# Tile-by-tile memory hand-over, early activation loads and a ScalarE permutation in a two-layer hybrid encoder

## The chip, the cores and the metric

The kernel runs on 1 core of one Trainium2 chip. The metric is the device time of one execution in microseconds (us). Traces come from the hardware profiler of that core. TensorE's clock has two granted levels, 2.4 GHz (1.00 in the tables) and 1.2 GHz.

## What is computed

Sixteen learned meta tokens are put ahead of 512 tokens, 528 in all, of width 2048, float32. Two layers follow, each with an RMSNorm in front and a residual add behind, and a last RMSNorm. Cut to what matters:

```
def even_layer(h, ...):
    proj = rmsnorm(h) @ w_in                     # 2048 x 12352
    z_a, xs, Bm, Cm, dt_f, dt_b, z_b, glu_v, glu_g = split_cols(proj)
    y_a = ssd_mixer(...)                         # conv 5, two-way chunked scan, gate z_a, norm
    y_b = conformer_conv(glu_v, glu_g) * silu(z_b)   # conv 31, LayerNorm
    return h + concat(y_a, y_b) @ w_out          # 4096 x 2048

def odd_layer(h, ...):
    q, k, v, z = split(rmsnorm(h) @ w_in)        # 2048 x 8192
    o = neighbourhood_attention(q, k, v, rpb)    # 8 rows x 64 columns, window 16 columns
    return h + (o * silu(z)) @ w_out             # 2048 x 2048
```

The attention layer keeps its tokens with the column of the grid first and the row second, so the first layer's result is permuted once, from (row, column) to (column, row).

## The kernel before, in words

Activations lie with the channels on the 128 partitions, 16 tiles of 128 x 528 per layer. Every product is computed to float32 accuracy by three matmuls: weights and activations are split into a rounded high part and a rest (`wh`, `wl`; `rh`, `rl`), and high x high, low x high and high x low are accumulated. `fetch` (line 214) splits a weight half-panel of 128 x 1024, ScalarE for `wh` (line 221), DVE for `wl` (line 224); weights are loaded by SP (line 145) into three buffers `raw`, and three split halves are kept ahead. `split` (line 277) makes `rh` on ScalarE and `rl` on DVE; the results live in a ring of 16 tiles each, so a new stage's tile k takes the place of the old stage's tile k.

The program is a row of stages:

- an input stage with the SSD heads (to about 1060 us), then the gate stage of lines 613 to 662: 16 panels of `z_b`, whose loop runs beside the LayerNorm of `ln` (line 623). Its tiles lie in the pools `zbp` (14 tiles), `big` (16) and `rp`; each product `xc` is stored to `yb_d`.
- three calls of `phase` (line 808): the output projection of `y_a` (from `yz_d`), that of `y_b` (from `yb_d`, with `done_b` at line 862, which adds the residual, permutes the tokens and stores to `h1_d`), and the q, k, v projection (from `h1_d`). A phase fills the ring by `fill` (line 696), does four panels by `proj`, and the rest two panels at a time as 7 half-size products instead of 8 by `sproj` (line 232), for which `combos` (line 713) makes sums of activation halves, `ta` and `tb`; these sums need the same 16 tiles a second time. `fourth` (line 735) replaces one half of the ring from `t4_d`.
- The phases' pools are opened at lines 684 to 688: `sr` with 8 tiles, through which every streamed activation, residual and fourth block passes (`stream`, line 690), `tr` for `ta` and `tb`, `wx` for weight sums `wy` and `wb`, and `ev` for results `cx`, `cy`. The first `fill` issues on SP, later streams on POOL.
- the attention stage (lines 917 to 1189), pools `ak` and `ap`: 16 head pairs, with the panels of the gate `z` interleaved in chunks (`chunks`, `filler`), and, in the last two pairs, with `reload` (line 1087) of the first twelve gated outputs from `o_d` and `refill` (line 1099), which splits them into the ring.
- the output stage (from line 1182), pools `op`, `fp` and `wf`: the last projection with its own `combos` (line 1192), whose inputs `srf` share seven buffers `rr` with the residuals, then the last norm and the store.

A pool of a later stage takes the memory of an earlier one. Before the change every instruction that first uses a pool waits until the pools whose memory it takes are done with all their tiles. Across most of the program the order on each engine is planned by the framework from a simulated time line, and instructions move far from where they are written; in the attention stage the order on TensorE, DVE, ScalarE and POOL is the written one (`manual_schedule`), while SP's DMA issues are still planned. Each engine's queue runs in order.

Of the kernel before, what the change touches and what calls it, by code (L numbers as in the profile page):

```python
# [12 lines left out]
F32 = mybir.dt.float32  # L13
# [4 lines left out]
P = 128  # L18
# [42 lines left out]
SRB = 8  # L61
# [17 lines left out]
def hybrid_encoder(ctx: ExitStack, tc: tile.TileContext, hT, win, wdt, wout, oin, oout, par, con,  # L79
# [15 lines left out]
    nc.scalar.dma_start(cst[:, CON["one"][0]:], con[:, CON["one"][0]:])  # L95

# [515 lines left out]

    with ExitStack() as c1:
        psb = c1.enter_context(tc.tile_pool(name="psc", bufs=1, space=bass.MemoryType.PSUM))
        zb = c1.enter_context(tc.tile_pool(name="zbp", bufs=14))
        big = c1.enter_context(tc.tile_pool(name="big", bufs=16))
        rp = c1.enter_context(tc.tile_pool(name="rp", bufs=1))
# [32 lines left out]
        for m in range(KT):  # L650
# [5 lines left out]
            if bgc:  # L656
                pump(bgc, 7000)
                if not bgc:
                    bgs.append(ln())
            else:  # L660
                pump(bgs, 7000)
        pump(bgs, 1e9)
# [20 lines left out]
    with ExitStack() as c1:  # L683
        sr = c1.enter_context(tc.tile_pool(name="sr", bufs=SRB))
        wx[1] = c1.enter_context(tc.tile_pool(name="pse", bufs=4, space=bass.MemoryType.PSUM))
        tr = c1.enter_context(tc.tile_pool(name="tr", bufs=KH))
        wx[0] = c1.enter_context(tc.tile_pool(name="wx", bufs=1))
        ev = c1.enter_context(tc.tile_pool(name="ev", bufs=1))

        def stream(src, q=nc.gpsimd):  # L690
            t = sr.tile([P, L], F32, name="srt", tag="srt")
            if src is not None:
                q.dma_start(t, src)
            return t

        def fill(src, g, q=nc.gpsimd):
            hs, ls = [], []
            for k in range(KT):
                t = src(k) if k in near else stream(src(k), q)
# [35 lines left out]
        def fourth(hs, ls):  # L735
            ts = deque()
            for k in range(0, KH + 4, 2):
                now = [ts.popleft() for _ in range(2 if k >= 4 else 0)]
                for kk in range(k, min(k + 2, KH)):
                    t = sr.tile([P, L], F32, name="sr4", tag="srt")  # L740
# [121 lines left out]
        def done_b(m, t, ps):  # L862
# [5 lines left out]
            if t is None:  # L868
                t = ev.tile([P, L], F32, name="cx", tag="xy", bufs=3)
                nc.scalar.activation(h2(t), ps, AF.Copy)  # L870
            nc.vector.tensor_tensor(r1[:, :NM], t[:, :NM], r0[:, :NM], op=ALU.add)
            nc.vector.tensor_tensor(r1[:, NM:].rearrange("p (c r) -> p r c", r=GR), t[:, NM:].rearrange("p (r c) -> p r c", r=GR),
                                    r0[:, NM:].rearrange("p (r c) -> p r c", r=GR), op=ALU.add)
# [43 lines left out]
    wx[0] = None  # L917
    pstack.close()
    psp[0] = pstack.enter_context(tc.tile_pool(name="pz", bufs=2, space=bass.MemoryType.PSUM))

    with ExitStack() as c2:
# [184 lines left out]
        with tc.manual_schedule(engines={eng.PE, eng.DVE, eng.Activation, eng.Pool}):  # L1106
# [15 lines left out]
            for p in range(KT):  # L1122
# [47 lines left out]
                if p == KT - 2:  # L1170
                    refill(0, 4)
# [234 lines left out]
```

## Time and profile before

| | us |
|---|---|
| three runs | 2688.16, 2694.21, 2695.9 (median 2694.21) |
| the profiled execution | 2690.2 |
| its span, first to last instruction | 2688.4 |
| TensorE busy | 2620.0 (97%) |
| DVE busy | 2056.2 (76%) |
| ScalarE busy | 1399.4 (52%) |
| POOL busy | 395.4 (15%) |

Times in the rows count from the start of the span. PE is TensorE's matmuls, PEld its weight loads, ACT ScalarE, SP the queue of SyncE, which only issues DMAs. Matmuls are pipelined, so the busy time of one overlaps the next: a gap between two starts says more than a sum of durations. What ended an idle time is inferred from semaphores.

### The profile page before, as it was taken

The page shows a single profiled execution, that of the slowest core. Times are in us where ns is not written, and L with a number is a line of the kernel's source. Part 1 is how long each engine was busy: PE and PEld are TensorE (multiplying, and loading weights), DVE is VectorE, ACT ScalarE, POOL GpSimd, SP SyncE. Part 2 cuts the span into 40 slices and gives each one's busy share as a digit, 9 for nine tenths or more (in the row PEclk, how much of TensorE's full clock was granted, in tenths as well). Part 3 has the DMA queues.
Part 4 walks back from the last instruction along what each step waited for, and adds up shares of the span by engine and source line. Part 5 has one row for each costly group of instructions (what it writes and reads, how often), then busy time and mean ns, then how long its engine had stood idle before and what let it go on. Part 6 is the DMA issues. An engine that isn't in the chain of part 4 may idle for free.

```text
span 2688.4 us, 52587 instructions
## 1 busy us (share of the span) xinstructions
PE 2620.0 (97%) x21228; PEld 2499.3 (93%) x21228; DVE 2056.2 (76%) x3019; ACT 1399.4 (52%) x2601; POOL 395.4 (15%) x608
## 2 busy tenths in 40 slices
PE   8999999999999999999899999999999999999997
PEld 7999999999999999999899989999999987777797
DVE  7775967888587969987588888877777766666776
ACT  5355585655658655225454445633333455566443
POOL 2000000000000001101121212200000042442432
PEclk9999999999999999999999999999999999999998
DMA  4222222232222223434776767755555453543764
GB/s 162 96 75 92 84 78 95 79 99 74 89 87 73 90 89 100 156 103 143 249 215 194 250 186 244 239 159 157 158 149 155 143 152 119 142 124 108 244 185 151
DMA packets 145156, 375.50 MB, mean 140 GB/s; under 512 B 32512, under 2 KB 45472, under 8 KB 144912
## 3 DMA queue, kind: packets, MB, share of 16 engines
q1 hardware_dynamic: 121296, 292.68, 33.8%
q0 software_dynamic: 23328, 79.38, 11.0%
q8 instruction: 167, 2.74, 0.4%
q14 instruction: 77, 0.63, 0.1%
q10 hardware_dynamic: 288, 0.07, 0.0%
HBM read 321.64 MB, written 50.43 MB: 138 GB/s over the span
## 4 chain that ended last, share of the span: by engine, by line
PE 79%; DMA 6%; DVE 6%; ACT 5%; issue 3%; POOL 1%; SPq 0%; DVEq 0%; POOLq 0%; ACTq 0%
PE ps L266 40%; PE pb L245 25%; PE ps L1059 6%; PE py L537 2%; DVE wl L224 1%; PE po L1045 1%; ACT wh L221 1%; DMA srt<-yz_d 1%; PE st L477 1%; DVE a L560 1%; PE pq L996 1%; DMA t_d<-srt 1%; DMA srt<-yb_d 1%; ACT T L505 1%; ACT L507 1%
## 5 line engine op out<-in xcount | busy, mean ns | idle before, releaser
L266 PE MATMUL ps<-rh,wh 128*128 128x264 f32 (+1 forms) x3520 | 732.2, 287 | 21.3 <-ACT rh L283 17.4
L266 PE MATMUL ps<-rh,wl 128*128 128x264 f32 (+1 forms) x3520 | 732.3, 287 | 0.4 <-DVE wl L224 0.4
L266 PE MATMUL ps<-rl,wh 128*128 128x264 f32 (+1 forms) x3520 | 727.6, 287 | 1.9 <-DVE rl L284 1.3
L221 ACT ACTIVATE wh<-raw 128x1024 fp32r<-128x1024 f32 (+1 forms) x341 | 360.4, 1057 | 530.7 <-PE ps L266 278.8
L266 PEld LDWEIGHTS ps<-rh,wh 128*128 128x128 f32 (+1 forms) x3520 | 550.5, 189 | 28.6 <-ACT rh L283 18.4
L224 DVE TENSOR_TENSOR wl<-raw,wh 128x1024 fp32r<-128x1024 f32 (+1 forms) x341 | 432.4, 1268 | 165.6 <-ACT wh L221 160.3
L266 PEld LDWEIGHTS ps<-rl,wh 128*128 128x128 f32 (+1 forms) x3520 | 547.4, 188 | 6.6 <-DVE rl L284 2.9
L266 PEld LDWEIGHTS ps<-rh,wl 128*128 128x128 f32 (+1 forms) x3520 | 550.4, 188 | 3.0 <-DVE wl L224 0.9
L245 PE MATMUL pb<-rh,wh 128*128 128x264 f32 (+1 forms) x1280 | 364.1, 285 | 1.3 <-DVE fo L1290 1.3
L245 PE MATMUL pb<-rl,wh 128*128 128x264 f32 (+1 forms) x1280 | 363.7, 284 | 0.0
L245 PE MATMUL pb<-rh,wl 128*128 128x264 f32 (+1 forms) x1280 | 363.0, 284 | 0.4 <-DVE wl L224 0.4
L560 DVE SCALAR_TENSOR_TENSOR a<-up,prm,a 128x528 f32<-128x528 f32 x464 | 343.9, 771 | 2.4 <-ACT a L555 1.0
L245 PE MATMUL pb<-ta,wh 128*128 128x264 f32 (+1 forms) x1280 | 241.4, 286 | 9.2 <-ACT wh L221 3.9
L245 PEld LDWEIGHTS pb<-rh,wh 128*128 128x128 f32 x1280 | 241.0, 188 | 2.4 <-DVE fo L1290 2.4
L245 PEld LDWEIGHTS pb<-rh,wl 128*128 128x128 f32 x1280 | 240.7, 188 | 0.8 <-DVE wl L224 0.8
L245 PEld LDWEIGHTS pb<-rl,wh 128*128 128x128 f32 x1280 | 240.9, 188 | 0.0
L245 PEld LDWEIGHTS pb<-ta,wh 128*128 128x128 f32 x1280 | 200.9, 190 | 11.3 <-ACT wh L221 4.9
L221 ACT ACTIVATE wh<-wy 128x1024 fp32r<-128x1024 f32 x117 | 123.9, 1059 | 147.9 <-PE pb L245 97.3
L224 DVE TENSOR_TENSOR wl<-wy,wh 128x1024 fp32r<-128x1024 f32 x117 | 146.0, 1248 | 61.1 <-ACT wh L221 61.0
L245 PE MATMUL pb<-ta,wl 128*128 128x264 f32 (+1 forms) x640 | 183.7, 287 | 5.3 <-DVE wl L224 5.3
L221 ACT ACTIVATE wh<-wb 128x1024 fp32r<-128x1024 f32 x80 | 84.7, 1059 | 99.5 <-PE pb L245 50.0
L245 PEld LDWEIGHTS pb<-ta,wl 128*128 128x128 f32 x640 | 121.5, 190 | 7.3 <-DVE wl L224 7.3
(328 smaller groups left out, 4149.6 us busy)
## 6 DMA issues: line engine op xcount, KB each, us to landing
raw<-win SPq DMA_DIRECT2D x192, 512.0 KB, 3.6
raw<-oin SPq DMA_DIRECT2D x84, 512.0 KB, 4.5
raw<-wout SPq DMA_DIRECT2D x40, 512.0 KB, 5.5
wb<-oin SPq DMA_DIRECT2D x22, 512.0 KB, 4.0
wy<-oin SPq DMA_DIRECT2D x22, 512.0 KB, 3.4
wy<-oin POOLq DMA_DIRECT2D x22, 512.0 KB, 7.6
raw<-oout SPq DMA_DIRECT2D x20, 512.0 KB, 4.9
srt<-h_d POOLq DMA_DIRECT2D x38, 264.0 KB, 4.9
```

The lines of the kernel that those rows point to most:

```text
L221: nc.scalar.activation(wh, raw, AF.Copy)
L224: nc.vector.tensor_tensor(wl, raw, wh.bitcast(F32), op=ALU.subtract)
L245: nc.tensor.matmul(o, w[:, k, :], u[:, lo:lo + n], start=(new and k == 0 and j == 0), stop=(k == KH - 1 and j == 2), skip_group_check=not new)
L266: nc.tensor.matmul(ps[:M, n, :N], w[:, k, :], u[:, lo + n * N:lo + (n + 1) * N], start=(kk == 0 and j == 0), stop=(kk == KT - 1 and j == 2))
L477: nc.tensor.matmul(st[:, :nd * 256], xb[:, c, 256:], xd[:, d0:d1].rearrange("p r x -> p (r x)"), start=True, stop=True)
L505: nc.scalar.activation(T[:, d, c * CH:(c + 1) * CH], pf[:CH, c // 3, (c % 3) * CH:(c % 3 + 1) * CH], AF.Relu, bias=fcol[:, c, d, hd:hd + 1 ...
L507: nc.scalar.activation(h2(cq[:, d]), pf[:, :, :HL], AF.Exp)
L537: nc.tensor.matmul(py[j * HD:(j + 1) * HD, c // 3, (c % 3) * CH:(c % 3 + 1) * CH], a, b, start=(q == 0), stop=(q == nt - 1))
L560: nc.vector.scalar_tensor_tensor(a, u[:, j:j + L], wv(j), a, op0=ALU.mult, op1=ALU.add)
L996: nc.tensor.matmul(pqs[a, w][:, :n], x[hs, w * P:(w + 1) * P], y[hs, st:st + n], start=(j == 0), stop=(j == 2))
L1045: nc.tensor.matmul(self.po[hs, w * P:(w + 1) * P], lt, rt, start=(q == 0), stop=(q == nq - 1))
L1059: nc.tensor.matmul(ps, w[:, k, :], u[:, lo:lo + S], start=(kk == 0 and j == 0), stop=(kk == KT - 1 and j == 2))
```

## The change

- All pools from the gate stage on are opened with waits tile by tile: a new tile waits only for what lay under it.
- The stream pool is divided: `sr` with 5 tiles is opened ahead of the gate stage at the other end of the memory, and `sr2` with 3 at the old place; `slot` takes the eight in turn. `sr` is closed after the three phases.
- At panel 13 of 16 of the gate stage, the first five `yz_d` tiles are loaded into `sr`, on SP; `fill` finds them in `ready`.
- `done_b` adds on DVE without a permutation, in place, and ScalarE makes the two copies that permute.
- In the last pair but one, `refill(0, 4)` is divided in two and moved ahead, behind the second weight split and behind the second half of the scores.

```
-SRB = 8
+SRB, SRC = 5, 3
...
+    def pool(**kw):
+        return tc.tile_pool(reuse_waits="tile", **kw)
...
+    sstack = ctx.enter_context(ExitStack())
+    sr = [sstack.enter_context(pool(name="sr", bufs=SRB, side="right"))]
+    srn = [0]
+
+    def slot(name="srt"):
+        i = srn[0] % (SRB + SRC) if len(sr) > 1 else 0
+        srn[0] += 1
+        return sr[i >= SRB].tile([P, L], F32, name=name, tag="srt")
+
+    def stream(src, q=nc.gpsimd):
+        t = slot()
+        if src is not None:
+            q.dma_start(t, src)
+        return t
+
+    ready = {}
...
-        zb = c1.enter_context(tc.tile_pool(name="zbp", bufs=14))
-        big = c1.enter_context(tc.tile_pool(name="big", bufs=16))
+        zb = c1.enter_context(pool(name="zbp", bufs=14))
+        big = c1.enter_context(pool(name="big", bufs=16))
...
+            if m == KT - 3:
+                for k in range(SRB):
+                    ready[k] = stream(yz_d[k], nc.sync)
...
-        sr = c1.enter_context(tc.tile_pool(name="sr", bufs=SRB))
-        wx[1] = c1.enter_context(tc.tile_pool(name="pse", bufs=4, space=bass.MemoryType.PSUM))
-        tr = c1.enter_context(tc.tile_pool(name="tr", bufs=KH))
+        sr.append(c1.enter_context(pool(name="sr2", bufs=SRC)))
+        wx[1] = c1.enter_context(pool(name="pse", bufs=4, space=bass.MemoryType.PSUM))
+        tr = c1.enter_context(pool(name="tr", bufs=KH))
...
-                t = src(k) if k in near else stream(src(k), q)
+                t = src(k) if k in near else ready.pop(k) if k in ready else stream(src(k), q)
...
-                    t = sr.tile([P, L], F32, name="sr4", tag="srt")
+                    t = slot("sr4")
...
-            nc.vector.tensor_tensor(r1[:, :NM], t[:, :NM], r0[:, :NM], op=ALU.add)
-            nc.vector.tensor_tensor(r1[:, NM:].rearrange("p (c r) -> p r c", r=GR), t[:, NM:].rearrange("p (r c) -> p r c", r=GR),
-                                    r0[:, NM:].rearrange("p (r c) -> p r c", r=GR), op=ALU.add)
+            nc.vector.tensor_tensor(r0, r0, t, op=ALU.add)
+            nc.scalar.activation(r1[:, :NM], r0[:, :NM], AF.Copy)
+            nc.scalar.activation(r1[:, NM:].rearrange("p (c r) -> p r c", r=GR), r0[:, NM:].rearrange("p (r c) -> p r c", r=GR), AF.Copy)
...
+    sstack.close()
...
                 low()
+                if p == KT - 2:
+                    refill(0, 2)
                 if nxt:
                     nxt.scores((1, 2))
+                    if p == KT - 2:
+                        refill(2, 4)
                     cur.mix(o)
...
-                if p == KT - 2:
-                    refill(0, 4)
```

The remaining lines of the diff give the same `pool(...)` to `psc`, `rp`, `wx`, `ev`, `pz`, `psd`, `ak`, `ap`, `pr`, `op`, `fp`, `psf` and `wf`.

## Rows read from the trace of the kernel before

**Rows 1.** The page's parts 1 and 4: TensorE's busy time, share of the span and instructions, and the shares by engine of the chain of work that ended last.

```profile
PE 2620.0 (97%) x21228; PEld 2499.3 (93%) x21228; DVE 2056.2 (76%) x3019; ACT 1399.4 (52%) x2601; POOL 395.4 (15%) x608
...
PE 79%; DMA 6%; DVE 6%; ACT 5%; issue 3%; POOL 1%; SPq 0%; DVEq 0%; POOLq 0%; ACTq 0%
```

**Rows 2.** Busy time by stretch. The columns are the stretch in us from the span's start, its length, the busy time (and instructions) of PE, PEld, DVE, ACT and POOL, the share of TensorE's full clock that was granted, the mean busy share of the DMA engines and what they moved in GB/s.

```profile
1290.00:1299.00 9.00, 7.34 (x62) 7.18 (x60) 4.16 (x6) 2.65 (x3) 0.00 (x0) 1.00 0.21 62
...
1297.00:1372.00 75.00, 65.03 (x509) 63.73 (x508) 56.79 (x97) 46.89 (x76) 20.10 (x36) 0.95 0.87 282
...
1309.00:1340.00 31.00, 29.14 (x233) 28.41 (x233) 22.28 (x39) 21.60 (x33) 8.33 (x14) 1.00 1.00 328
...
1370.00:1460.00 90.00, 90.00 (x740) 90.00 (x739) 73.08 (x87) 34.54 (x38) 7.96 (x12) 1.00 0.62 181
...
1490.00:1536.00 46.00, 43.73 (x352) 43.06 (x353) 36.71 (x63) 20.42 (x32) 11.24 (x21) 1.00 0.77 254
...
1496.00:1680.00 184.00, 176.59 (x1408) 174.70 (x1408) 154.08 (x222) 86.96 (x123) 37.19 (x65) 0.98 0.70 219
...
1536.00:1580.00 44.00, 36.96 (x266) 35.29 (x265) 35.29 (x55) 18.85 (x30) 9.88 (x17) 0.92 0.63 198
...
2535.00:2565.00 30.00, 24.14 (x169) 22.72 (x168) 24.86 (x35) 13.81 (x23) 18.38 (x21) 0.89 0.73 226
```

**Rows 3.** Timeline around the end of the gate stage and the start of the first output projection, one row each of DVE, SP's DMA queue, ScalarE, TensorE and ScalarE again. The columns are start and duration in us, engine, line, operation, out<-in, shapes and count; in brackets the idle time before it and what ended it. Rows with a count merge several instructions.

```profile
1298.53 0.70 DVE L646 TENSOR_TENSOR xc<-xc,zb 128x528 f32<-128x528 f32 x1
...
1299.30 4.46 SPq L693 DMA_DIRECT2D srt<-yz_d  x8
...
1303.73 0.73 ACT L283 ACTIVATE rh<-srt,prm 128x528 fp32r<-128x528 f32 x1 [6.26 <-DMA srt<-yz_d]
...
1304.52 1.25 PE L266 MATMUL ps<-rh,wh 128*128 128x264 f32 x4 [7.18 <-ACT rh L283]
...
1325.96 0.74 ACT L283 ACTIVATE rh<-srt,prm 128x528 fp32r<-128x528 f32 x1 [0.38 <-DMA srt<-yz_d]
```

**Rows 4.** The second output projection: the instructions of lines 871, 872, 851 and 846 (durations are minimum/median/maximum in ns, then the first and last start in us); one row of the waits from 1536 to 1580 us (us in total, times, longest); and the row of TensorE's timeline with its longest wait there.

```profile
L871 DVE TENSOR_TENSOR srt<-cx,srt x10: 167/169/175, 1500.0 to 1670.1; 128x16 f32<-128x16 f32 x10
...
L872 DVE TENSOR_TENSOR srt<-cx,srt x10: 1144/1196/1209, 1500.0 to 1670.2; 128x512 f32<-128x512 f32 x10
...
L851 DVE TENSOR_TENSOR srt<-srt,cx x6: 701/702/703, 1378.3 to 1492.3; 128x528 f32<-128x528 f32 x6
...
L846 ACT ACTIVATE cx<-ps x4: 587/592/593, 1330.3 to 1356.8; 128x528 f32<-128x528 f32 x4
...
ACT sq L881 <- DVE srt L872: 5.6, 2, 2.8
...
1549.92 0.51 PE L245 MATMUL pb<-ta,wh 128*128 128x264 f32 x2 [2.45 <-ACT wh L221]
```

**Rows 5.** Around the change to the attention stage: timeline rows of TensorE, POOL, DVE, TensorE and DVE, and between them the stretch from 2172 to 2179 us with the columns of rows 2.

```profile
2165.54 0.28 PE L245 MATMUL pb<-ta,wl 128*128 128x264 f32 x1
...
2168.82 0.80 POOL L930 MEMSET bm<- 128x16 f32 x16 [48.05 <-PE pb L245]
...
2172.00:2179.00 7.00, 4.67 (x22) 3.57 (x21) 4.02 (x12) 2.65 (x6) 6.27 (x9) 0.76 0.99 255
...
2173.94 0.81 DVE L958 TENSOR_TENSOR ql<-tq,qh 128x512 fp32r<-128x512 f32 x1
...
2174.81 0.36 PE L996 MATMUL pq<-kh,ql 64*128 64x208 f32 x2 [2.33 <-DVE ql L958]
...
2177.28 0.38 DVE L1001 CUSTOM_DVE_ANT_0 sb<-pq,bm 128x208 f32<-128x208 f32 x1 [2.53 <-DMA vqk_d<-cy]
```

**Rows 6.** Around the last refills: the first DMA issue of line 1096 (durations in ns, first and last start in us), the stretch from 2470 to 2490 us, DVE's weight split in the timeline, two rows of the chain of work in order of time (start and duration in us, what, count), TensorE's timeline row after it, and, for comparison, a TensorE row at the start of the second output projection.

```profile
L1096 SPq DMA_DIRECT2D accl<-o_d x1: 319/319/319, 2248.2 to 2248.2; - x1
...
2470.00:2490.00 20.00, 15.05 (x103) 11.78 (x100) 14.44 (x33) 12.31 (x27) 2.95 (x2) 0.83 0.19 67
...
2469.89 1.23 DVE L224 TENSOR_TENSOR wl<-raw,wh 128x1024 fp32r<-128x1024 f32 x1 [2.07 <-ACT wh L221]
...
2473.13 0.50 ACT sb L1002 x2
...
2477.28 3.71 DVE rl L281 x4
...
2481.49 1.17 PE L1020 MATMUL pa<-cst,sb 128*128 128x128 f32 x4 [4.95 <-DVE sb L1009]
...
1495.96 0.51 PE L266 MATMUL ps<-rh,wh 128*128 128x264 f32 x2 [1.40 <-ACT rh L280]
```

**Rows 7.** Around the output stage: timeline rows of DVE, POOL, DVE and twice TensorE, and a row of the chain of work in a later stretch without a break.

```profile
2490.25 2.48 DVE L281 TENSOR_TENSOR rl<-ord,rh 128x512 fp32r<-128x512 f32 x4
...
2502.41 1.14 POOL L1237 DMA_DIRECT2D rr<-h_d  x2 [23.18 <-DMA o_d<-o]
...
2506.23 0.43 DVE L1198 TENSOR_TENSOR srf<-srf 128x256 f32<-128x256 f32 x1 [6.89 <-DMA srf<-o_d]
...
2537.65 0.39 PE L245 MATMUL pb<-ta,wh 128*128 128x256 f32 x1 [2.01 <-ACT ta L1209]
...
2546.50 0.39 PE L245 MATMUL pb<-ta,wh 128*128 128x256 f32 x1 [1.70 <-DVE ta L1210]
...
2578.58 19.82 PE pb L245 x167
```

More of the change, by code (lines that the diff above doesn't have):

```diff
@@ L611, in hybrid_encoder @@
         pump(bgs, 1e9)
+    sstack = ctx.enter_context(ExitStack())
[11 more added lines that the diff above has]
+    ready = {}
     with ExitStack() as c1:
-        psb = c1.enter_context(tc.tile_pool(name="psc", bufs=1, space=bass.MemoryType.PSUM))
-        zb = c1.enter_context(tc.tile_pool(name="zbp", bufs=14))
-        big = c1.enter_context(tc.tile_pool(name="big", bufs=16))
-        rp = c1.enter_context(tc.tile_pool(name="rp", bufs=1))
+        psb = c1.enter_context(pool(name="psc", bufs=1, space=bass.MemoryType.PSUM))
+        zb = c1.enter_context(pool(name="zbp", bufs=14))
+        big = c1.enter_context(pool(name="big", bufs=16))
+        rp = c1.enter_context(pool(name="rp", bufs=1))
         mu = accl
@@ L683, in hybrid_encoder @@
     with ExitStack() as c1:
-        sr = c1.enter_context(tc.tile_pool(name="sr", bufs=SRB))
-        wx[1] = c1.enter_context(tc.tile_pool(name="pse", bufs=4, space=bass.MemoryType.PSUM))
-        tr = c1.enter_context(tc.tile_pool(name="tr", bufs=KH))
[L687 to L694, printed above, removed]
+        sr.append(c1.enter_context(pool(name="sr2", bufs=SRC)))
+        wx[1] = c1.enter_context(pool(name="pse", bufs=4, space=bass.MemoryType.PSUM))
+        tr = c1.enter_context(pool(name="tr", bufs=KH))
+        wx[0] = c1.enter_context(pool(name="wx", bufs=1))
+        ev = c1.enter_context(pool(name="ev", bufs=1))
         def fill(src, g, q=nc.gpsimd):
@@ L917, in hybrid_encoder @@
     wx[0] = None
+    sstack.close()
     pstack.close()
-    psp[0] = pstack.enter_context(tc.tile_pool(name="pz", bufs=2, space=bass.MemoryType.PSUM))
+    psp[0] = pstack.enter_context(pool(name="pz", bufs=2, space=bass.MemoryType.PSUM))
     with ExitStack() as c2:
-        psb = c2.enter_context(tc.tile_pool(name="psd", bufs=1, space=bass.MemoryType.PSUM))
-        ak = c2.enter_context(tc.tile_pool(name="ak", bufs=1))
-        ap = c2.enter_context(tc.tile_pool(name="ap", bufs=1))
+        psb = c2.enter_context(pool(name="psd", bufs=1, space=bass.MemoryType.PSUM))
+        ak = c2.enter_context(pool(name="ak", bufs=1))
+        ap = c2.enter_context(pool(name="ap", bufs=1))
         am = cn("am").rearrange("p (w c) -> p w c", w=NWIN)
@@ L1182, in hybrid_encoder @@
     with ExitStack() as c3:
-        psr = c3.enter_context(tc.tile_pool(name="pr", bufs=1, space=bass.MemoryType.PSUM))
-        op = c3.enter_context(tc.tile_pool(name="op", bufs=NRES))
-        fp = c3.enter_context(tc.tile_pool(name="fp", bufs=1))
-        wx[1] = c3.enter_context(tc.tile_pool(name="psf", bufs=4, space=bass.MemoryType.PSUM))
-        wx[0] = c3.enter_context(tc.tile_pool(name="wf", bufs=1))
+        psr = c3.enter_context(pool(name="pr", bufs=1, space=bass.MemoryType.PSUM))
+        op = c3.enter_context(pool(name="op", bufs=NRES))
+        fp = c3.enter_context(pool(name="fp", bufs=1))
+        wx[1] = c3.enter_context(pool(name="psf", bufs=4, space=bass.MemoryType.PSUM))
+        wx[0] = c3.enter_context(pool(name="wf", bufs=1))
         SH = S // 2
```

## Prediction

> **What bounds the kernel now.** I read the page first: TensorE is busy 97% of the span, and the chain that ended last runs on it for 79% [rows 1]. An engine that full leaves only its holes to be won, so the next view is the table of busy time by stretch [rows 2]. In the steady stage from 1370 to 1460 us it issues 740 matmuls in 90 us, 0.1216 us each. Against that pace three stretches fall short. 1297 to 1372 us has 509 matmuls, worth 61.9 us in 75: 13.1 lost. 1536 to 1580 us has 266, worth 32.3 in 44: 11.7 lost. 2535 to 2565 us has 169 narrower ones; at 0.119 us (167 took 19.82 us without a break [rows 7]) they are worth 20.1 in 30: 9.9 lost. The timelines show two more holes, of 2.33 and 4.95 us, each with matmuls at half speed behind it. The five hold some 46 us, 1.7% of the span, and all lie where one stage hands its memory or its inputs to the next. So the question is which of the five the change closes.
>
> **First hand-over (1297 us).** The reader is to see the order of events [rows 3]. DVE ends the last `xc` product at 1299.2; only then does SP issue the first eight `yz_d` loads. ScalarE gets the first tile at 1303.73, TensorE starts at 1304.52 after 7.18 us of idleness, and at a mean granted clock of 0.95 over the 75 us, 7.5 us of them ran at 1.2 instead of 2.4 GHz. The loads go on until ScalarE splits the last tile at 1325.96. The data in `yz_d` were not late: the wait is for memory, since pool `sr` waits for all of the pools that lay there.
>
> Afterwards five tiles stand in a pool beside `zbp` and `big`, not over them, and are loaded at panel 13 of 16, some 23 us before the end. Eight issues took 4.46 us, so five take 2.8 us of SP. They stand ahead of weight loads, which run three halves ahead of use; I cost them at nothing, and at 2.8 us without that lead. Tiles 5 to 7 go where `gp` lay, done long before; 8 to 15 follow as splits free the slots. A ring slot is free once the last panel has read it, and eight splits (0.73 us each on ScalarE, about as much on DVE) fit beside that panel: DVE is busy 4.16 of the last 9 us [rows 2]. Then TensorE can go straight on. The best is the whole 13.1 us. I take 10, since the last tiles and the first combinations must still arrive; the lower end is 4.1, by the first rival.
>
> **Token permutation.** In `done_b` DVE does an add of 16 columns (0.17 us) and a permuting one (1.19); afterwards it does one flat add, like line 851 at 0.70 [rows 4]. That is 0.66 us less, 16 times: 10.6 us of DVE. ScalarE gets two copies each time. No row shows a permuting copy there. The nearest is a flat copy of 528 columns at 0.59 us, and DVE's permuting form costs 1.7 times its flat one, so a pair costs between 0.6 and 1.4 us; I take 1.2, as one side is strided. That is 19 us on an engine busy for 87 of 184 us there [rows 2], beside TensorE as long as the weight splits that stand behind the copies keep their lead. The store to `h1_d` and the square then wait for 0.7 + 1.2 instead of 1.36 us, half a microsecond later, with nobody on TensorE's path behind them. DVE's saving counts only where DVE sets the pace: in the second stretch it is busy for 35 of 44 us, and TensorE's longest wait there is 2.45 us for a weight split [rows 2, 4]. Four tiles precede it, 2.6 us, with a little of the half-speed time behind it. I take 3. The ends are 8 and, because the order there is planned anew, a loss of 3.
>
> **Into the attention stage (2170 us).** POOL's clearing of `bm` starts at 2168.82, when TensorE is done with everything; `ql` ends at 2174.75, for which TensorE waits 2.33 us [rows 5]. The granted clock is 0.76 over the 7 us around it, another 1.7 us. With waits tile by tile `kh` and `ql` lie over `ta` tiles, whose last matmul stands at 2165.54, three microseconds earlier. I take 3.8 of the 4.0; the lower end is nothing. Next in line is the first maximum (line 1001), which waits 2.53 us for a store out of `ev`; it will lie over weight tiles, so that goes too, and TensorE has chunks of `z` to work on meanwhile.
>
> **Refills.** In the last pair but one DVE runs four `rl` splits in 3.71 us from 2477.28, behind ScalarE's gate work, and only then the scaling that TensorE's transposes wait for, idle for 4.95 us [rows 6]. At a granted 0.83 over 20 us, 6.8 us were at half speed; 2.4 of them fell into the wait, so 4.4 cost 2.2. Together 7.1. Their inputs need no new wait: the first reload was issued at 2248. Moved, two splits follow DVE's weight split (ended at 2471.1) and push the maxima and the exponentials, which now end at 2473.6, back by 1.2 us; two more on ScalarE (1.1 us) and the last on DVE end at about 2476.9. The scaling starts there instead of at 2480.99, and the hole shrinks to about 1 us. A wait of 1.40 us elsewhere, in a stretch at a granted 1.00, had no half-speed time behind it [rows 2, 6]. I take 5.8; the ends are 2.2 and 7.1.
>
> **Output stage (2535 us).** Loads into the last pools wait until the final `o` tile is stored: POOL's first residual is issued at 2502.41 after 23.18 us, and the first combination starts at 2506.23 after 6.89 us in which DVE had nothing [rows 7]. From there on each combination comes too late for TensorE, which waits for `ta` at 2537.65 and 2546.50, partly at the low clock. Afterwards the seven `rr` tiles lie over `bm` and over `kh` and `kl` copies, last read by a split that ends at 2492.7, so loading can begin some 9 us earlier, and a lead of 9 us covers these waits. I take 8.5 of the 9.9; the lower end is 4, by the first rival.
>
> **Sum.** 10 + 3 + 3.8 + 5.8 + 8.5 = 31.1 us. The pools of the gate stage from 1060 us have no hole to close: nothing. The profiled execution took 2690.2 us, so 2659.1. The median of the three runs is 4.0 us higher; the same saving from there gives 2663.1. I predict 2661. The lower ends add up to 7.3 us and the upper ends to 42.1; with some of each, this case alone runs from 2649 to 2677.
>
> **Rivals.** *Transfers set the pace.* From 1309 to 1340 us the DMA engines are at a share of 1.00 and 328 GB/s [rows 2]. If that, and not the wait for memory, sets the pace, the five early tiles (5 x 264 KB = 1.35 MB) return 4.1 us, and the output stage (share 0.73) perhaps 4: 4.1 + 3 + 3.8 + 5.8 + 4 = 20.7, or 2672 us. For it: the share. Against it: from 1290 to 1299 us the same engines are at 0.21, and that is what earlier waits would fill. Chance 0.18. The Trainium skill, page Trainium Kernel Development and Optimization, section Key Constraints, states that DMAs from the SP, ACT and POOL queues run on the same 16 DMA engines, and that several queues save issue time alone; by it, what is loaded earlier must fit into time in which those engines stand idle, and no run here shows yet how much does.
>
> *The waits do not come apart*, because what lay under a new tile is itself among the last in use. Then the attention and output stages return nothing, the first hand-over 4.1 and the refills 5.8: 2682 us. Against it stand the tile sizes in the code, by which `kh` and `rr` lie away from the last users. Chance 0.11.
>
> *Slower: ScalarE's queue.* In each of 16 `done_b` ScalarE now stands at a copy until DVE's add is done, with weight splits behind it. Its square stands there already, 2.8 us at the longest [rows 4]. If 16 such holds reached TensorE whole, they would cost 45 us against the 31 gained: 2706. It decides only from where a hold exceeds the lead of the weight splits; two blocks of 24 matmuls are 5.8 us. Chance 0.05. Another 0.06 is for gains that a newly planned order of instructions hands back: 2690.
>
> **How the numbers follow.** The forecast has 0.60. The range from 2645 to 2682 takes it in, with the first rival and the edge of the second. A measurement of this kernel tells 0.3%, 8 us, from no change. The forecast, the first rival and most of the second are faster: 0.87. The rest of the second and the handed-back gains are the same: 0.08. Slower: 0.05.
>
> **What would show it.** Right: `yz_d` tiles issued before 1275 us, no hole over 2 us near 1297, no half-speed stretch at 2175 and 2480 us, the first `srf` load before 2497. Wrong: TensorE waiting for `yz_d` tiles 8 to 15 at a DMA share near 1, `bm` still cleared after the last matmul, `o_d` still ahead of the first residual, or `wh` late behind the new copies between 1490 and 1680 us.

## The result, and the profile after

The changed kernel takes 2666.73 us (median of five runs, 2665.1 to 2668.85), the kernel before 2691.37 on the same chip: a ratio of 0.9906 with a 95% interval from 0.9891 to 0.992. The forecast was 2661, with a range from 2645 to 2682. The profiled execution took 2666.49 us against 2690.2. So the direction and the rough size came as forecast; the terms of the sum did not all.

First the page of the kernel after, parts 1 and 4 (as [rows 1]):

```profile
PE 2612.9 (98%) x21228; PEld 2494.8 (94%) x21228; DVE 2050.5 (77%) x3003; ACT 1416.8 (53%) x2633; POOL 390.7 (15%) x608
...
PE 82%; DVE 5%; ACT 5%; DMA 3%; issue 3%; POOL 0%; DVEq 0%; SPq 0%; POOLq 0%; ACTq 0%
```

TensorE runs the same 21228 matmuls in a span of 2664.1 us where it was 2688.4. It idles 17 us less (51.2 for 68.4) and is busy 7 us less, with a mean granted clock of 0.992 where it was 0.989. To see where, I set the k-th matmul of one trace against the k-th of the other (21228 in each; TensorE's order differs by small exchanges alone) and took the difference of their start times at a few places. The table is worked out, not a view: us gained on the profiled execution of the kernel before, between those matmuls that there start at the times in the heading, up to the start of the last one. Each row is one execution.

```
us of before:     0-1290  -1372  -1460  -1580  -2150  -2300  -2440  -2492  -end   all
the change          0.89  13.35  -0.01   2.61   0.84  -3.88   0.08   3.63  6.09  23.59
e1_scan_pools       1.00  13.35  -0.04   2.44   0.32  -1.09  -0.10   3.55  6.31  25.75
e2_entry_pools      0.10  13.36  -0.06   2.13  -3.48  -5.60  -0.04   3.59  6.26  16.26
e3_out_pools        0.94  13.36  -0.04   0.41  -0.38  -3.87   0.01   3.59  1.77  15.79
e4_waits_only       1.23  -2.31  -0.00  -0.33   0.58   0.75   0.00  -0.55  4.76   4.13
e5_no_early        -0.89  13.36  -0.03   2.00  -1.53  -2.54  -0.07   3.55  6.27  20.11
e6_perm_dve        -0.32  13.35  -0.02   1.74  -0.73  -0.57  -0.03   3.60  5.81  22.84
e7_second_gate      0.26  13.35  -0.02   1.03   1.00   0.95  -0.01   3.57  6.02  26.16
e8_refill_late      0.05  13.35   0.00  -1.14   1.71  -2.55   0.04  -0.60  5.66  16.52
e9_out_pool         0.62  13.35  -0.02  -0.28  -0.18  -1.02  -0.01   3.59  4.02  20.08
e10_mul_dve         0.25  13.35   0.02   1.47   0.61  -0.55   0.06   1.70  4.88  21.79
e11_all             0.16  13.35  -0.01  -0.66   0.61  -1.80  -0.05   1.86  4.97  18.43
e12_chunk_first     0.13  13.35  -0.01   0.86   2.04  -4.64   1.19   3.60  7.09  23.60
```

The columns behind 1290 and 2440 repeat to a tenth of a microsecond where nothing was changed in them. Those from 1460 to 2300 scatter by 2 to 5 us between kernels that are alike there, so in them a single profile settles little. The columns named in what follows: hand-over (1290 to 1372), permutation (1460 to 1580), entry (2150 to 2300), refills (2440 to 2492), output (from 2492).

Busy time by stretch of the kernel after, columns as in [rows 2]:

```profile
1286.00:1297.00 11.00, 11.00 (x93) 11.00 (x92) 11.00 (x17) 9.81 (x16) 3.12 (x6) 1.00 0.95 327
1297.00:1358.00 61.00, 61.00 (x504) 61.00 (x503) 47.88 (x85) 37.77 (x63) 18.32 (x33) 1.00 0.86 285
...
1520.00:1540.00 20.00, 14.74 (x87) 13.18 (x86) 17.52 (x30) 10.04 (x19) 6.51 (x13) 0.83 0.64 206
2154.00:2161.00 7.00, 4.06 (x23) 3.12 (x21) 5.08 (x12) 3.97 (x10) 4.34 (x4) 0.75 0.94 261
2450.00:2470.00 20.00, 18.76 (x132) 14.03 (x131) 13.63 (x37) 15.00 (x36) 3.81 (x4) 1.00 0.33 108
2510.00:2545.00 35.00, 32.00 (x228) 29.91 (x227) 30.38 (x45) 17.38 (x29) 18.80 (x21) 0.95 0.77 239
```

The hand-over is without a hole and at the full clock: 504 matmuls in 61 us, where [rows 2] have 509 in 75. What is left lies at 1520, at 2154 and at 2510 us.

**Hand-over.** SP's DMA queue and ScalarE in the timeline, which answer to [rows 3]:

```profile
1069.23 2.28 SPq L628 DMA_DIRECT2D srt<-yz_d  x5
...
1194.27 1.33 SPq L628 DMA_DIRECT2D srt<-yz_d  x3
...
1286.33 5.02 SPq L628 DMA_DIRECT2D srt<-yz_d  x7
...
1284.27 0.72 ACT L286 ACTIVATE rh<-srt,prm 128x528 fp32r<-128x528 f32 x1
...
1299.41 0.74 ACT L286 ACTIVATE rh<-srt,prm 128x528 fp32r<-128x528 f32 x1 [1.70 <-DMA srt<-yz_d]
```

Eight of the sixteen tiles are issued 90 to 220 us before they are needed, the other eight from 1286 us as splits free their slots, and the last split begins at 1299.41 where it was 1325.96 before.

**Permutation.** ScalarE's new copies, from the groups of instructions between 1460 and 1670 us (busy time, mean ns of one, idle time before them):

```profile
L890 ACT ACTIVATE srt<-srt 128x512 f32<-128x512 f32 x16 | 19.6, 1247 | 0.0
...
L889 ACT ACTIVATE srt<-srt 128x16 f32<-128x16 f32 x16 | 3.5, 216 | 8.5 <-DVE srt L888 8.5
```

A pair takes 1.46 us, just above the upper end of my estimate (1.4).

**Entry.** Timeline rows of ScalarE, POOL, DVE and TensorE (as [rows 5]), and two of pair 1 behind them:

```profile
2151.03 1.06 ACT L224 ACTIVATE wh<-raw 128x1024 fp32r<-128x1024 f32 x1 [1.87 <-PE pb L248]
2151.99 0.64 ACT L971 ACTIVATE kh<-accl 128x544 fp32r<-128x544 f32 x1
...
2145.70 0.15 POOL L948 MEMSET bm<- 128x16 f32 x2 [9.21 <-PE pb L248]
...
2148.65 9.69 POOL L996 TENSOR_TENSOR bm<-cst,prm 128x64 f32<-128x64 f32 x12
...
2155.29 1.27 DVE L976 TENSOR_TENSOR kl<-accl,kh 128x544 fp32r<-128x544 f32 x1
2156.49 1.24 DVE L976 TENSOR_TENSOR ql<-tq,qh 128x512 fp32r<-128x512 f32 x1
...
2157.78 0.54 PE L1014 MATMUL pq<-kh,ql 64*128 64x208 f32 x2 [2.94 <-DVE ql L976]
...
2183.71 4.91 DVE L227 TENSOR_TENSOR wl<-raw,wh 128x1024 fp32r<-128x1024 f32 x1 [2.07 <-ACT wh L224]
...
2170.95 16.59 POOL L996 TENSOR_TENSOR bm<-cst,bt 128x64 f32<-128x64 f32 x32
```

POOL clears `bm` from 2135.44 on and is done with it before TensorE's last matmul of the stage before (2150.83), as the tile waits were to allow. TensorE waits all the same, 2.94 us where it was 2.33: for `ql`, which DVE makes behind a weight split, a scaling and `kl` without a pause. POOL's first bias, 9.69 us from 2148.65, now runs beside all of this; `kl` and `ql` take 1.27 and 1.24 us where [rows 5] have 0.81 for `ql`.

**Refills.** TensorE, DVE, POOL and TensorE (as [rows 6]):

```profile
2463.28 0.87 PE L1038 MATMUL pa<-cst,sb 128*128 128x128 f32 x4 [0.66 <-DVE sb L1027]
...
2464.12 3.19 DVE L1027 TENSOR_SCALAR sb<-sb,sm 128x208 f32<-128x208 f32 x4
...
2464.47 2.72 POOL L1099 TENSOR_TENSOR o<-o,z 128x512 f32<-128x512 f32 x2 [24.63 <-ACT z L1097]
...
2473.97 0.50 PE L1077 MATMUL ps<-rl,wh 128*128 128x512 f32 x1 [1.42 <-DVE rl L284]
```

The hole of 4.95 us is down to 0.66. But the second scaling now takes 3.19 us beside POOL's gate products, and TensorE waits 0.58 (at 2469.49) and 1.42 us for the refills behind it.

**Output.** POOL, SP's queue, DVE and TensorE (as [rows 7]):

```profile
2467.13 1.15 POOL L1257 DMA_DIRECT2D rr<-h_d  x2
...
2481.34 0.44 SPq L1216 DMA_DIRECT2D srf<-o_d  x1
...
2485.84 0.42 DVE L1218 TENSOR_TENSOR srf<-srf 128x256 f32<-128x256 f32 x1 [3.99 <-DMA srf<-o_d]
...
2525.14 0.39 PE L248 MATMUL pb<-ta,wh 128*128 128x256 f32 x1 [1.24 <-DVE ta L1230]
2526.70 0.58 PE L248 MATMUL pb<-ta,wh 128*128 128x256 f32 x1 [1.05 <-ACT ta L1229]
```

The residuals go out 35 us earlier than in [rows 7] and the first combination 20 us earlier; the whole program has moved by 17.5 us there, so 18 and 3 us are the output stage's own. Before, TensorE waited four times for `ta` (2.01, 0.55, 1.70 and 1.05 us); the first two waits are gone, the third is 1.24 and the last is still 1.05 us.

### The profile page after: what moved, and what is told of

The parts are those of the page before. It is cut to its first block, busy times and chain, and to the rows that moved or that the text cites. A ratio compares the mean times of both kernels' runs of the same rounds, so it can differ in the third digit from the quotient of the medians.

```text
span 2664.1 us, 52574 instructions
## 1 busy us (share of the span) xinstructions
PE 2612.9 (98%) x21228; PEld 2494.8 (94%) x21228; DVE 2050.5 (77%) x3003; ACT 1416.8 (53%) x2633; POOL 390.7 (15%) x608
## 4 chain that ended last, share of the span: by engine, by line
PE 82%; DVE 5%; ACT 5%; DMA 3%; issue 3%; POOL 0%; DVEq 0%; SPq 0%; POOLq 0%; ACTq 0%
PE ps L269 42%; PE pb L248 26%; PE ps L1077 6%; PE py L540 2%; DVE wl L227 1%; ACT wh L224 1%; PE st L480 1%; PE po L1063 1%; DVE a L563 1%; PE pq L1014 1%; DMA srt<-h_d 1%; ACT T L508 1%; DMA srt<-yb_d 1%; ACT L510 1%; ACT sb L1020 1%
## 5 line engine op out<-in xcount | busy, mean ns | idle before, releaser
L227 DVE TENSOR_TENSOR wl<-raw,wh 128x1024 fp32r<-128x1024 f32 (+1 forms) x341 | 434.7, 1275 | 161.9 <-ACT wh L224 157.0
```

Of the source, the lines that this page charges most:

```text
L227: nc.vector.tensor_tensor(wl, raw, wh.bitcast(F32), op=ALU.subtract)
```

## The experiments

Ratios are against the kernel before, run beside each kernel; the changed kernel's is 0.9906 [0.9891, 0.992]. Runs of one kernel lie up to 11 us apart, so differences of 2 us are read from the traces.

**What the hand-over needs.** Three kernels. The first keeps everything but the tile waits of that part:

```
-        psb = c1.enter_context(pool(name="psc", ...))      # and nine more pools
+        psb = c1.enter_context(tc.tile_pool(name="psc", ...))
```

> The changed kernel with the waits by whole pools again for the ten pools of the first hand-over and the two stretches after it (sr, sr2, psc, zbp, big, rp, pse, tr, wx, ev); the early yz_d loads and the rest of the change stay, and every engine's instructions keep their order. Theory A (the loads are early only because the tile waits let them be): the first yz_d no longer lands before 1280 us, the idle stretch ahead of the first split matmul comes back at 4 to 7 us with a half-speed clock behind it, and the time is 2673 to 2684 us, 6 to 17 over the changed kernel's 2667. Theory B (the place in SP's queue three panels ahead does it by itself): 2665 to 2670 us, and no idle stretch over 2 us near 1297 us. If the early loads now block SP's queue for the weights behind them, it is over 2690.

2667.4 us, 0.9903 [0.9888, 0.9918]. Theory B: the hand-over gains the same 13.35 us. With whole-pool waits the first five loads go out at 1076.56 instead of 1069.23, which is still 200 us early.

The second leaves out the loop of early loads:

```
-            if m == KT - 3:
-                for k in range(SRB):
-                    ready[k] = stream(yz_d[k], nc.sync)
```

> The changed kernel without the loop that issues the first five yz_d loads three panels ahead; the five tiles stay in their own pool beside the others, the tile waits stay, and the loads are issued where the stage fills its inputs. Theory A (what gains is the place of the tiles, since nothing that is still in use lies under them): the loads still go out before 1290 us, no idle stretch over 2 us at the hand-over, 2665 to 2670 us. Theory B (the loop three panels ahead is needed): the loads go out behind the last weights at about 1290 to 1298 us, the hand-over loses 6 to 13 us again, 2673 to 2680 us.

2670.25 us, 0.9917 [0.9903, 0.993]; the profiled execution gains 13.36 us at the hand-over. Theory A, with a time a quarter of a microsecond over its range. SP's queue in its timeline:

```profile
1071.02 2.28 SPq L628 DMA_DIRECT2D srt<-yz_d  x5
```

The planned order puts these loads on SP some 215 us before the first split, whether the program asks for them at panel 13 or where the stage fills its inputs. The third is the kernel before with tile waits alone:

```
-        sr = c1.enter_context(tc.tile_pool(name="sr", bufs=SRB))      # and 17 more pools
+        sr = c1.enter_context(tc.tile_pool(reuse_waits="tile", name="sr", bufs=SRB))
```

> The kernel before with tile waits for all pools that the change touches, and nothing else of the change: eight sr tiles in one place, yz_d loaded where it was, the permutation on DVE, the refills in one piece. Theory A (the parts are separate: the first hand-over needs the early load, the output stage only the waits, and the entry loses to them): output +6.4, entry -3.8, hand-over 0 to 4, so 2685 to 2689 us against 2691. Theory B (tile waits alone bring the yz_d loads forward as well): another 8 to 13 less, 2672 to 2680 us.

2681.67 us, 0.9962 [0.9949, 0.9975]. In its profile the hand-over loses 2.31 us instead of gaining; the rows of SP and TensorE look like [rows 3]:

```profile
1297.48 4.72 SPq L693 DMA_DIRECT2D srt<-yz_d  x8
...
1303.51 1.25 PE L266 MATMUL ps<-rh,wh 128*128 128x264 f32 x4 [7.41 <-ACT rh L283]
```

So the hand-over and the output stage are separate as theory A had it, though the time is 3 us under its range: the profiled execution, 2685.77, is the slowest of five, and where the faster ones gained their 4 us no trace shows. The place of the tiles closes the hole: with it, the loop can go or the tile waits can go (no run leaves out both); without it, tile waits do not help. The entry did not come as theory A had it; this kernel's rows there stand with the next experiment.

**The attention's waits.**

```
-    psp[0] = pstack.enter_context(pool(name="pz", ...))      # and psd, ak, ap
+    psp[0] = pstack.enter_context(tc.tile_pool(name="pz", ...))
```

> The changed kernel with waits by whole pools again for the four pools of the attention alone (pz, psd, ak, ap); all orders stay. Theory A (at the entry the tile waits cost 3.8 us: they let POOL start on the bias while DVE still makes kl and ql, so that these take 1.25 us each and not 0.8 to 1.0, and POOL is late for pair 1): kl and ql are back at 0.8 to 1.0 us, POOL's first bias waits until TensorE is done, and the time is 2661 to 2665 us, 2 to 6 under 2667. Theory B (the loss at the entry comes from the order of the ScalarE and DVE work there, whatever POOL does): 2666 to 2669 us. Theory C, as my prediction had it (the tile waits gain at the entry, and the loss lies in the pairs after it): 2669 to 2672.

2667.01 us, 0.9897 [0.988, 0.9915], the same time as with tile waits and in theory B's range. `kl` and `ql` are back at 0.99 and 0.81 us, as theory A expected, and TensorE's wait at 2.33, so theory A's mechanism is there, and its gain is 0.6 us. The runs lie far apart (2662.79 to 2673.64); the profiled one is the slowest, with a longer collision in pair 1 than any other kernel's:

```profile
2162.79 0.36 PE L1014 MATMUL pq<-kh,ql 64*128 64x208 f32 x2 [2.33 <-DVE ql L976]
...
2186.13 7.52 DVE L227 TENSOR_TENSOR wl<-raw,wh 128x1024 fp32r<-128x1024 f32 x1 [2.07 <-ACT wh L224]
```

So in the changed kernel the tile waits of the attention neither gain nor cost anything that shows in the time, and theory C falls. In e4, the kernel before with tile waits, they do gain. TensorE, POOL and DVE there:

```profile
2174.41 0.36 PE L996 MATMUL pq<-kh,ql 64*128 64x208 f32 x2 [1.09 <-DVE ql L958]
...
2156.74 8.79 POOL L978 TENSOR_TENSOR bm<-cst,prm 128x64 f32<-128x64 f32 x12
...
2173.68 0.68 DVE L958 TENSOR_TENSOR ql<-tq,qh 128x512 fp32r<-128x512 f32 x1
```

TensorE waits 1.09 us where the kernel before has 2.33 and the changed one 2.94, and 2.77 us are gained up to 2185 us, with the clock at 1.00 where it was 0.76. `kh` starts as long after TensorE's last matmul of the stage before as in the other two (1.2 us). What differs is POOL: its first bias is over at 2165.53, and DVE's last five instructions up to the end of `ql` take 3.69 us, against 4.94 in the kernel before and 5.55 in the changed one, where POOL runs beside them. These differences are those of the waits. In the changed kernel POOL clears the last of `bm` 2.6 us ahead of TensorE's last matmul, in e4 12.6 us ahead; that this comes from the new place of the stream pool is likely, but no run shows it.

In e1, whose attention is that of the changed kernel to the last wait, the same stretch ran at the full clock with TensorE as idle (4.07 us busy of 7) as at 0.75 in the changed kernel:

```profile
2154.00:2161.00 7.00, 4.07 (x29) 3.16 (x28) 5.61 (x12) 3.73 (x10) 4.94 (x4) 1.00 0.99 270
```

From 2150 to 2185 us e1 gains 0.91 us and the changed kernel loses 2.07. With every engine's order the same, the 3 us between them are the clock, which fell behind this hole in one execution and not in the other.

**The collision in pair 1.** POOL's bias of pair 2 waits for pair 1's scaling:

```
-                if p == 0:
+                if p < 2:
                     cur.norm(0)
                     cur.norm(1)
                     gate = ...
                     nc.gpsimd.tensor_copy(gate, cur.sb[1][:, NWIN - 1, 0:1])
...
-                if p:
+                if p > 1:
```

> The changed kernel in which POOL's bias of pair 2 waits for the end of pair 1's scaling on DVE, as that of pair 1 already waits for pair 0's; one tiny copy on POOL more, nothing else. In the changed kernel POOL runs on from pair 1 into pairs 2 and 3, and a weight split of DVE that starts meanwhile takes 4.91 us and not 1.2 to 1.8. Theory A (the split stands because POOL works beside it): that split takes under 2 us, the transposes of pair 1 no longer wait, and some 2 us come back: 2663 to 2666 us. Theory B (something else holds that split, its input for example): it stays at 4 to 7 us, and the time is 2666 to 2669. If pair 2's bias is now late for its own maxima: over 2669.

2665.5 us, 0.9904 [0.9889, 0.9919]. DVE's weight split and POOL in its timeline:

```profile
2182.77 1.23 DVE L227 TENSOR_TENSOR wl<-raw,wh 128x1024 fp32r<-128x1024 f32 x1 [2.07 <-ACT wh L224]
...
2170.14 7.83 POOL L996 TENSOR_TENSOR bm<-cst,bt 128x64 f32<-128x64 f32 x12
2188.16 0.18 POOL L1148 COPY gate<-sb 128x1 f32<-128x1 f32 x1 [10.19 <-DVE sb L1027]
```

Theory A: with POOL at rest the split takes 1.23 us instead of 4.91, and the loss of 1.8 us behind it is gone (0.04 us gained from 2185 to 2300 us). e11 and e12, which have the same gate, show 1.23 as well. Without the gate the collision comes in most executions, not in all: the split took 1.64 us in e6 and 1.36 in e10. The medians lie 1.2 us apart, which the runs alone would not show.

**The refills.**

```
-                if p == KT - 2:
-                    refill(0, 2)
...
-                    if p == KT - 2:
-                        refill(2, 4)
...
+                if p == KT - 2:
+                    refill(0, 4)
                 next(g)
```

> The changed kernel with the four refills of the last pair but one in one piece behind the gate work again; the rest stays. Theory A (spreading them is worth 3.5 us net: the hole of 5 us before the scaling closes, but the scaling then meets POOL's gate products, takes 3.2 us instead of 1.1, and the next refills are 2.6 us later): 2669 to 2672 us; in this kernel the hole is back at 4 to 5 us, the scaling takes about 1.1 us, and the next refills make TensorE wait for less than 1 us in all. Theory B, as my prediction had it (5.8 us, nothing handed back): 2672 to 2674 us. Theory C (the stage behind it absorbs either): 2666 to 2668 us.

2673.92 us, 0.9933 [0.9921, 0.9946]. TensorE's hole and DVE's second scaling:

```profile
2469.97 1.17 PE L1038 MATMUL pa<-cst,sb 128*128 128x128 f32 x4 [4.94 <-DVE sb L1027]
...
2470.81 1.11 DVE L1027 TENSOR_SCALAR sb<-sb,sm 128x208 f32<-128x208 f32 x4
```

The trace is as theory A had it: the hole of 4.94 us is back, the scaling takes 1.11 us, no wait for `rl` follows. In the table the refills and the output stage differ by 4.7 us from the changed kernel's. The medians differ by 7.2, and the time is in theory B's range; but the profiled execution also has 3.8 us of scatter at the permutation, and by the table the size lies between A and B. Then POOL's two products on DVE:

```
-                    (nc.gpsimd if q < KT - 2 else nc.vector).tensor_tensor(os_[q], os_[q], zts[q], op=ALU.mult)
+                    (nc.gpsimd if q < KT - 4 else nc.vector).tensor_tensor(os_[q], os_[q], zts[q], op=ALU.mult)
```

> The changed kernel with the gate products of heads 12 and 13 on DVE and not on POOL, where they run beside the last scaling; the other engines' instructions stay as they are. Theory A (the scaling takes 3.2 us and not 1.1 because POOL's products run beside it, and so the next refills come 2.5 us late): the scaling is back at 1.1 us, TensorE's waits of 0.6 and 1.4 us for rl go or shrink, DVE has 1.4 us more to do, net 1 to 2.5 us gained, 2664 to 2666 us. Theory B (DVE is the bound there, whoever else works): the products on DVE cost 1 to 2 us, 2668 to 2669.

2671.27 us, 0.9927 [0.9913, 0.994]. Slower than either theory gave, and both are right in part. DVE and TensorE:

```profile
2465.74 1.11 DVE L1027 TENSOR_SCALAR sb<-sb,sm 128x208 f32<-128x208 f32 x4
...
2464.89 1.17 PE L1038 MATMUL pa<-cst,sb 128*128 128x128 f32 x4 [3.61 <-DVE sb L1027]
```

The scaling is back at 1.11 us and the waits for `rl` are gone, so POOL's work did stretch it; but the products stand ahead of the first scaling, behind ScalarE's gates, and open a hole of 3.61 us. The refills gain 1.70 in place of 3.63 us, the output stage 4.88 in place of 6.09.

**The output stage.**

```
-        op = c3.enter_context(pool(name="op", bufs=NRES))      # and pr, fp, psf, wf
+        op = c3.enter_context(tc.tile_pool(name="op", bufs=NRES))
```

> The changed kernel with waits by whole pools again for the five pools of the output stage alone (pr, op, fp, psf, wf); all orders stay. Theory A (the 6.4 us that the output stage gained are those of the tile waits, by the residuals and the first o_d reloads that no longer wait for the store of the last gated tile to land): 2671 to 2675 us, and the residual loads on POOL are again issued after 2490 us. Theory B (the output stage gains because the refills leave ScalarE and DVE free earlier): 2666 to 2669 us.

2671.37 us, 0.992 [0.9906, 0.9933]. Theory A in time and place (the residuals' time less so: 2486.69, not after 2490). POOL and DVE:

```profile
2486.69 1.16 POOL L1257 DMA_DIRECT2D rr<-h_d  x2 [16.02 <-DMA o_d<-o]
...
2492.25 0.42 DVE L1218 TENSOR_TENSOR srf<-srf 128x256 f32<-128x256 f32 x1 [6.92 <-DMA srf<-o_d]
```

The output stage gains 1.77 in place of 6.09 us: 4.3 are those of the tile waits, as e4 has it by itself (4.76). The rest may be held by SP's queue:

```
-                nc.sync.dma_start(x, o_d[k])
-                nc.sync.dma_start(y, o_d[KH + k])
+                q = nc.gpsimd if k < 2 else nc.sync
+                q.dma_start(x, o_d[k])
+                q.dma_start(y, o_d[KH + k])
```

> The changed kernel with the first four reloads of gated tiles in the output stage (srf, two pairs) issued by POOL behind its first residual, and not by SP, in whose queue they stand behind a weight load and two stores of gated tiles until 2481 us. Theory A (the order of SP's queue is what still holds the output stage): POOL issues them some 10 us earlier, the first combination comes 2 to 4 us earlier against the matmuls, the waits for ta of 1.5 and 1.3 us near 2530 us shrink, and the time is 2662 to 2665 us. Theory B (DVE's refills set the first combination, not the loads): 2665 to 2668 us and the waits for ta stay. Theory C (POOL issues more slowly, and its later residuals come late): over 2669.

2669.28 us, 0.9914 [0.9901, 0.9927]. POOL in the timeline, SP's load in the chain of work that ended last, and TensorE:

```profile
2477.10 0.56 POOL L1217 DMA_DIRECT2D srf<-o_d  x1 [7.94 <-issue]
...
2482.78 6.84 DMA srf<-o_d
...
2529.28 0.77 PE L248 MATMUL pb<-tb,wh 128*128 128x256 f32 x2 [3.05 <-DVE fo L1306]
```

The time is theory C's, though not by its cause. POOL begins its loads some 6 us earlier against the matmuls, not 10, since it first waits 7.94 us. The order was planned anew, and the chain runs through a load that SP issues at 2482.78 and that takes 6.84 us to land; DVE's first combination waits for it. TensorE's waits for `ta` do shrink, to one of 0.42 us, but 3.05 us for a result `fo`, which DVE reaches late in its new order, take their place (3.06 in e11). The first combination comes some 2 us later against the matmuls, not earlier, so A and B are not told apart: what caps the output stage stays open.

**The permutation back on DVE.**

```
-            nc.vector.tensor_tensor(r0, r0, t, op=ALU.add)
-            nc.scalar.activation(r1[:, :NM], r0[:, :NM], AF.Copy)
...
+            nc.vector.tensor_tensor(r1[:, :NM], t[:, :NM], r0[:, :NM], op=ALU.add)
...
```

> The changed kernel with the token permutation of the second stretch inside DVE's add again, as before the change; the rest stays, though the order of the instructions of that stage is planned anew. Theory A (the move to ScalarE is worth the 2.6 us that the stretch from 1460 to 1580 us gained): 2668 to 2671 us. Theory B (the stretch gained because its inputs come earlier, and the move is worth nothing): 2665 to 2668 us. Theory C (the ScalarE copies cost more than they give, in the 9.7 us still lost between 1520 and 1540): under 2665 us.

2669.77 us, 0.9918 [0.9905, 0.9932], by its time within theory A. But its profile still gains 1.74 us at the permutation, and kernels that have the copies on ScalarE gain between -1.14 and 2.61 there. The intervals overlap. Inconclusive; no sign of theory C.

**Together.** The edits of e7, e9 and e10:

> The changed kernel with three edits together: POOL's bias of pair 2 behind the scaling of pair 1, the first four reloads of the output stage on POOL, and the gate products of heads 12 and 13 on DVE. If the three places are separate and theory A holds for each, 2 + 3 + 1.5 us come off: 2659 to 2662 us. If only the second gate gains: 2664 to 2666 us.

2671.65 us, 0.9927 [0.9915, 0.9939]: neither. The second gate removes its collision. The refills gain 1.86 us, about as in e10, and the output stage 4.97, no worse than in e9 (4.02) or e10 (4.88) alone.

**More work at the entry.** The second gate, and one block of z matmuls moved:

```
             cur.values()
+            next(g)
             cur.scores((0, 3))
...
-                next(g)
+                if p != 6:
+                    next(g)
                 if nxt:
                     nxt.scores((0, 3))
```

> The kernel with the second gate (POOL's bias of pair 2 behind pair 1's scaling), and at the entry of the attention one block of 12 z matmuls more ahead of the first scores; the block is taken from pair 7, between its value transposes and its first scores, where TensorE has not waited. Theory A (at the entry TensorE lacks other work while ScalarE's kh and DVE's kl and ql are made, one after the other, whatever the waits for memory): the hole of 3.3 us ahead of the second group of score matmuls shrinks to under 0.7 us, the half-speed stretch behind it goes, and 2.5 to 4 us come off: 2661 to 2664 us. Theory B (the chain is only put off: the exponentials, the scaling and the transposes of pair 0 are then late by as much): 2665 to 2668 us. If pair 7 misses its block, a new hole of up to 2.8 us stands near 2260 us.

2667.55 us, 0.9915 [0.9901, 0.993]. TensorE's three waits and DVE ahead of the second:

```profile
2159.16 0.36 PE L1014 MATMUL pq<-kh,ql 64*128 64x208 f32 x2 [0.22 <-DVE ql L976]
...
2227.97 0.69 DVE L1088 TENSOR_TENSOR z<-ps,rs 128x512 f32<-128x512 f32 x1 [4.98 <-POOL o L1099]
...
2229.35 1.30 PE L1038 MATMUL pa<-cst,sb 128*128 128x128 f32 x4 [2.35 <-DVE sb L1027]
...
2272.18 1.16 PE L1038 MATMUL pa<-cst,sb 128*128 128x128 f32 x4 [2.41 <-DVE sb L1027]
```

The mechanism of theory A is shown: with 12 matmuls more ahead of the scores, TensorE's wait for `ql` is 0.22 us in place of 2.94. The time is not: each z is now evacuated a block earlier, DVE stands 4.98 us until POOL's product frees one of the three z buffers, and two new holes of 2.35 and 2.41 us eat the gain. Pair 7 itself leaves no hole where it lost its block. A fourth z buffer wasn't tried.

No kernel here beats the changed one beyond doubt; e7 is as fast or a microsecond faster.

## Why the prediction was right, and where it was not

**Hand-over: forecast 10, measured 13.35.** The mechanism is the forecast's: the wait was for memory, and what counts is that the tiles lie beside `zbp` and `big`. Mis-sized was the deduction of 3 us for the last tiles and the first combinations. I had the loads going out 23 us ahead; they go out 90 to 220 us ahead, so eight splits and the second eight loads fit beside the last panels (DVE busy 11.00 of 11 us there, TensorE too). The first rival, that transfers set the pace, is refuted here: at a DMA share of 0.95 no matmul waits.

**Permutation: 3 against 2.61**, with a scatter as large as the term. A copy pair costs 1.46 us, not 1.2, and is mostly hidden: TensorE waits 0.63 us (at 1525.16) for a `cx` that ScalarE makes behind one, and whether the waits after it hang on the same pair is not shown. DVE still is busy 17.5 of 20 us at 1520, where TensorE now loses time that it lost later before; the size of this term is not settled.

**Entry: 3.8 against -3.9.** This is the step that failed. It read [rows 5] so that `kh` and `ql` are late because their memory is. In the trace after, the memory is free and `bm` cleared early, and TensorE waits as long: `kh` stands behind the last `wh` in ScalarE's order, which is written by hand, and `kl` and `ql` stand behind two other instructions in a DVE that does not pause. By e2 the waits gain nothing in the changed kernel, by e12 other work for TensorE closes the hole. That e4 gains 2.77 us here with the waits alone is no rescue of the step: there too `kh` starts no earlier, and the gain comes by POOL, which was out of DVE's way, and by the clock. Most of the loss is not the change's: it is 2.07 us up to 2185 us, where e1 gains 0.91 with the same instructions at the full clock, and 1.81 behind it from the collision with POOL, which e2 and e4 have too and e7 takes away. The 0.6 us by which the wait for `ql` grew is the change's own.

**Refills: 5.8 against 3.63.** The hole shrank as worked out (to 0.66, forecast about 1) and the half-speed stretch went. Missing was what is late next: the scaling, moved forward, meets POOL's gate products, and 2.0 us (0.58 and 1.42) return as late refills (e8, e10).

**Output: 8.5 against 6.09.** Cause and direction are shown (e3, e4). The forecast took it that a lead of 9 us covers all waits; it covers two of the four, since the reloads stand in SP's queue until 2481 us and land 4 us after DVE wants them. Whether the queue or the landing sets this is open.

The five terms sum to 21.8 against a forecast of 31.1; the other 1.8 us of the table lie where nothing was forecast. The total is nearer than its terms by luck: four of them were forecast 12.65 us too high, and the hand-over, 3.35 too low, and those 1.8 us made up for part of it. The second rival's 2682 leaves out the 3 us of the permutation, which its condition does not touch; with them it is 2679. Of the signs named ahead, four came (loads before 1275, no hole at 1297, no half-speed stretch at 2480, first `srf` before 2497) and one did not (half speed at the entry).

The Trainium skill, page SBUF — State Buffer, section Who interferes with whom, states that a DVE instruction with two SBUF inputs and a GpSimd instruction that reads SBUF exclude each other. The trace agrees with it in kind: 4.91 us beside POOL, 1.23 without. How long the one that is late may have to wait is another matter (below).

## What to carry to other kernels

Where a stage starts with a wait for memory, first ask what lies under its first tiles: a place that nothing late has used closed the hole whole, with or without finer waits. Before a late operand is put down to memory, look whether the engine that makes it stood idle or was working through its queue; in the second case finer waits do not bring its result forward by themselves, and other work for the waiting engine closes the hole, though in e12 two new ones opened behind it. When work is moved forward, look at what the other engines do at the new place: two of the five terms here were cut by POOL running beside DVE, and at the entry the same waits gained (e4) or did not (the changed kernel) by whether POOL was done in time.

## What was not expected of the hardware

A DVE instruction may wait for more than the POOL instruction that is under way. In the kernel after, the split of 4.91 us ends at 2188.62, 1.08 us after the last of POOL's run (2170.95 + 16.59 = 2187.54): about its undisturbed length after POOL paused, with nine POOL instructions begun meanwhile. In the kernel before, the same split beside POOL's run got in between:

```profile
2199.33 1.74 DVE L224 TENSOR_TENSOR wl<-raw,wh 128x1024 fp32r<-128x1024 f32 x1 [2.07 <-ACT wh L221]
```

In the 14 traces that place has 1.23 us in the three kernels with the second gate, where POOL rests, and in the others 1.36, 1.64, 1.74, 2.78, six times 4.91 to 5.07, and 7.52. It is one source of the spread between runs.
